# Transposes and eight column tiles of a later projection beside the first token mixing, dense rounds of eight chunks, other gather rates

## The chip, the cores and the metric

The kernel runs on one core of a Trainium2 chip. The metric is the device time of one execution in microseconds (us), the median of several runs. The engines are TensorE (PE in the rows, with its weight loads as PEld), VectorE (DVE), ScalarE (ACT), GpSimd (POOL) and SyncE (SP), and 16 DMA engines move data between HBM and the on-chip memories SBUF and PSUM. "Clock" is the TensorE clock that the chip granted, as a share of full speed.

## The reference, cut

One decoder layer over 1024 tokens of width 1024, in float32:

```python
x = layer_norm(x)                                    # ln_in
proj = x @ w_in                                      # 3592 columns: fq fk fv ff hq hf hi hg
fox = causal_softmax(fq fk^T / 8 + c_t - c_s) @ fv   # 8 heads of 64, c = cumsum(log_sigmoid(ff))
hgrn = gated recurrence(hq, hf, hi)                  # 4 heads, 128x128 state, chunkwise
mix = concat(rms(fox), rms(hgrn) * silu(hg)) @ w_out
x = layer_norm(alpha * x + mix)                      # ln_mix
q = (x @ w_q)                                        # 8 heads x 2 halves x 128
s = q . sub_keys                                     # 128 scores per half
idx, best = top16(top16(s half 0) + top16(s half 1)) # of 128*128 experts, per head
gates = softmax(best)                                # 8 heads x 16 = 128 experts a token
h = gelu(x . u_tab[idx]) * gates
y = sum over the 128 experts of h * v_tab[idx]
return layer_norm(alpha * x + y)                     # ln_ffn
```

## The kernel before

**Precision.** A large product is three float32r matmuls: an operand is split into a hi part (a copy by ACT, float32r) and a lo part (raw minus hi, by DVE or POOL), and `mm3` (L281) issues hi*hi, hi*lo and lo*hi. `weight` (L204) loads a 128x1024 slice of weights into `wraw` on SP's queue, lets ACT make `whi`, and lets DVE or, by a counter and `WDIV`, POOL make `wlo`.

**Groups of tokens.** `mixers` (L311) goes through three groups: tokens 0 to 255, 256 to 767 and 768 to 1023. The first group's x is layer-normed, transposed and projected alone (T = 256); then comes its chain, `fox` and `hgrn`, the output projection with its layer norm `mix_out`, and the selection of experts, `select` and `select_tail`. Only then are the 768 later tokens projected, all at once: `project` (L407) transposes x from four tiles that `preload` had loaded (six tiles of 128 tokens, each eight 128x128 transposes by PE, hi by ACT and lo by DVE or POOL), and `project_cols` (L434) makes 17 column tiles m (24 matmuls of 512 columns and 24 of 256 each, by `projT`, evacuated by ACT at L451) and six groups of `wn` (`projN`, evacuated at L482). Then follow the second and the third group's chains, mixes and selections.

**Experts in two ways.** Tokens of blocks 0, 1, 6 and 7 (`GATHER`) fetch their experts' rows one by one: `gather_rows` (L1090) is an indirect DMA that POOL issues, 128 rows of 1024 (0.524 MB), into one of eight buffers `rows`. In `gather_u` (L1109) DVE multiplies such a row by x and sums it into `sd`; in `gather_v` DVE adds h times the row to `ys` in SBUF (L1134) for the blocks of `VDVE`, 1, 6 and 7, and for block 0 PE does the sum in PSUM. That is 512 u rows, 384 v rows on DVE and 128 on PE. Tokens of blocks 2 to 5 (`DENSE`) go through all 16384 experts in 128 chunks of 128: `up` (L1020) loads a chunk of u, splits it (uh by ACT, ul by DVE), makes the scores, gelu, multiplies by the gates `gt`, which `gbuild` had written to HBM, and splits into hh and hl; `down` (L1037) loads the chunk's v in two halves of 512 columns, splits (vh, vl), and sums into PSUM over a round of `JG` = 4 chunks; at a round's end DVE adds the four accumulators to `dy` (L1049). A round's `down` runs beside the next round's `up`.

**What sets the order.** The gathers are jobs that `tick` (L175) pulls forward: each stage of the program calls `tick` at its steps, and the table `RATE` says how many u rows, v rows and steps of `gbuild` a call pulls. In the dense part a tick is a chunk, 5.4 rows each; ticks of the first round, which stands over the last selection's tail, count `W0` = 0.71. `HOLD` holds the u rows back for some ticks after the first tail. From the program a scheduler makes one fixed order for each engine, and each engine runs its own in that order.

**PSUM.** One tile `y` of 128x1024 in the pool `psy` (single buffer) serves the sums on PE of block 0; `psf`, `psh` and `psv` are the other banks.

## Time and profile before

| | us |
|---|---|
| three runs | 3128.02, 3137.72, 3138.84 |
| median | 3137.72 |
| the profiled execution, whole | 3098.22 |
| its span on the core | 3096.5 |

The mean granted clock in the profiled execution is 0.918. From the start of the span the stages are, in us:

| stage | from | to |
|---|---|---|
| layer norm and projection of the first group | 0 | 123 |
| its chain, mix and layer norm | 123 | 239 |
| its selection and tail | 239 | 358 |
| transposes of the later x | 303 | 335 |
| projection of 768 tokens | 337 | 589 |
| second group | 589 | 1042 |
| third group: chain | 1042 | 1263 |
| mix, selection, gate build | 1263 | 1521 |
| dense part | 1521 | 3076 |
| last layer norm and store | 3076 | 3096.5 |

In the rows, a busy time in a stretch is the time in which an engine had at least one instruction; "x" is a count; "<-" names what released a wait. A timeline row has start, duration, engine, line, operation, output <- inputs and shapes.

### The profile page before, as it was taken

What the parts mean: (1) busy time and instruction counts of PE and PEld (TensorE: products, weight loads), DVE (VectorE), ACT (ScalarE), POOL (GpSimd) and SP (SyncE); (2) the same over time, 40 slices, a digit from 0 to 9 for tenths busy, and PEclk for the clock granted to TensorE, in tenths of its full rate; (3) what the DMA queues carried; (4) which work ended last, traced back from release to release, by engine and by line L of the source; (5) the groups of instructions that cost most, each with busy time, mean ns of one, the idle gap of its engine ahead of it and who ended that gap; (6) DMA issues with size and microseconds to landing.
All of it is one profiled execution on the core that took longest, in us unless ns stands there. A gap on an engine that the chain in (4) does not pass through costs nothing.

```text
span 3096.5 us, 45624 instructions
## 1 busy us (share of the span) xinstructions
PE 2614.4 (84%) x16057; PEld 2150.2 (69%) x16057; DVE 2707.3 (87%) x5573; ACT 1097.2 (35%) x2028; POOL 1678.8 (54%) x1240
## 2 busy tenths in 40 slices
PE   6778799777779768777569999899989999999995
...
DMA  7632599754978858763489999999999999999994
GB/s 269 198 137 89 184 336 330 241 162 151 350 253 290 290 164 298 256 249 144 186 280 342 346 377 360 340 366 361 350 344 367 381 379 357 357 370 342 370 336 159
DMA packets 338662, 887.13 MB, mean 286 GB/s; under 512 B 29912, under 2 KB 124136, under 8 KB 336000
## 3 DMA queue, kind: packets, MB, share of 16 engines
...
q8 instruction: 126, 2.06, 0.3%
...
## 4 chain that ended last, share of the span: by engine, by line
DVE 40%; PE 36%; issue 11%; DMA 6%; ACT 4%; POOL 3%; SPq 0%; DVEq 0%; POOLq 0%; ACTq 0%
DVE ys L1134 8%; DVE rows L1109 6%; PE psf L284 6%; PE psf L285 5%; PE psf L283 5%; PE psh L285 4%; PE psh L283 4%; PE psh L284 4%; DMA rows<-in_v,gsel 2%; POOL rows L1090 2%; DVE dy L1049 2%; DVE vl L1017 1%; DVE ohj L947 1%; DVE tw L793 1%; DVE al L947 1%
## 5 line engine op out<-in xcount | busy, mean ns | idle before, releaser
L1090 POOL DMA_INDIRECT rows<-in_u,gsel x512 | 689.7, 1347 | 481.8 <-DVE rows L1109 302.5
L1090 POOL DMA_INDIRECT rows<-in_v,gsel x512 | 637.9, 1246 | 433.3 <-DVE ys L1134 264.5
L1109 DVE SCALAR_TENSOR_TENSOR rows<-rows,gx 128x1024 f32<-128x1024 f32 x512 | 629.8, 1278 | 38.6 <-DMA rows<-in_u,gsel 25.3
L1134 DVE SCALAR_TENSOR_TENSOR ys<-rows,sd,ys 128x1024 f32<-128x1024 f32 x381 | 491.2, 1289 | 0.6
L283 PE MATMUL psh<-dxh,uh 128*128 128x512 f32 x1024 | 402.8, 393 | 28.9 <-ACT uh L1016 16.1
L285 PE MATMUL psh<-dxh,ul 128*128 128x512 f32 x1024 | 400.8, 391 | 9.5 <-DVE ul L1017 9.4
L284 PE MATMUL psh<-dxl,uh 128*128 128x512 f32 x1024 | 400.3, 391 | 0.0
L284 PE MATMUL psf<-vl,hh 128*128 128x512 f32 x768 | 312.3, 407 | 42.9 <-DVE vl L1017 42.1
L1016 ACT ACTIVATE vh<-vr 128x512 fp32r<-128x512 f32 x256 | 161.8, 632 | 435.8 <-PE psv L285 408.7
L285 PE MATMUL psf<-vh,hl 128*128 128x512 f32 x768 | 307.7, 401 | 0.0
L283 PE MATMUL psf<-vh,hh 128*128 128x512 f32 x768 | 279.1, 395 | 11.9 <-DVE dy L1049 9.7
L1016 ACT ACTIVATE uh<-ur 128x1024 fp32r<-128x1024 f32 x128 | 136.0, 1062 | 410.6 <-PE psh L284 408.9
L213 POOL TENSOR_TENSOR wlo<-wraw,whi 128x1024 fp32r<-128x1024 f32 x70 | 181.8, 2603 | 154.1 <-ACT whi L210 145.7
L283 PEld LDWEIGHTS psh<-dxh,uh 128*128 128x128 f32 x1024 | 193.5, 189 | 76.8 <-ACT hs L1030 20.3
L285 PEld LDWEIGHTS psh<-dxh,ul 128*128 128x128 f32 x1024 | 193.4, 189 | 50.6 <-DVE ul L1017 10.5
L210 ACT ACTIVATE whi<-wraw 128x1024 fp32r<-128x1024 f32 x130 | 136.9, 1056 | 250.8 <-PE psf L284 64.1
L284 PEld LDWEIGHTS psh<-dxl,uh 128*128 128x128 f32 x1024 | 193.6, 189 | 39.7
L284 PEld LDWEIGHTS psf<-vl,hh 128*128 128x128 f32 x768 | 148.7, 194 | 90.2 <-DVE vl L1017 59.4
L1017 DVE TENSOR_TENSOR vl<-vr,vh 128x512 fp32r<-128x512 f32 x256 | 170.6, 688 | 14.0 <-ACT vh L1016 13.9
L283 PEld LDWEIGHTS psf<-vh,hh 128*128 128x128 f32 x768 | 145.5, 190 | 50.1 <-DVE dy L1049 10.0
L213 DVE TENSOR_TENSOR wlo<-wraw,whi 128x1024 fp32r<-128x1024 f32 x60 | 81.8, 1365 | 111.0 <-ACT whi L210 111.0
L285 PEld LDWEIGHTS psf<-vh,hl 128*128 128x128 f32 x768 | 149.1, 194 | 30.2
(337 smaller groups left out, 6354.4 us busy)
## 6 DMA issues: line engine op xcount, KB each, us to landing
ur<-in_ut SPq DMA_DIRECT2D x128, 512.0 KB
vr<-in_v SPq DMA_DIRECT2D x256, 256.0 KB
...
```

The source lines that it names most:

```text
L210: nc.scalar.activation(hi, raw, AF.Copy)
L213: eng.tensor_tensor(lo, raw, hi.bitcast(F32), op=ALU.subtract)
L283: mm(out, lh, rh, start=start, stop=False, **kw)
L284: mm(out, lh, rl, start=False, stop=False, **kw)
L285: mm(out, ll, rh, start=False, stop=stop, **kw)
L947: eng.tensor_tensor(t.rearrange("p t (m c) -> p t m c", c=2), x, y, op=op)
L1016: nc.scalar.activation(hi, raw, AF.Copy)
L1017: nc.vector.tensor_tensor(lo, raw, hi.bitcast(F32), op=ALU.subtract)
L1049: nc.vector.tensor_tensor(y[:, tb, ns], y[:, tb, ns], acc[tb], op=ALU.add)
L1090: self.nc.gpsimd.indirect_dma_start(out=t, out_offset=None, in_=tab, in_offset=bass.IndirectOffsetOnAxis(ap=idx, axis=0))
L1109: self.pin(nc.vector.scalar_tensor_tensor(u, u, 1.0, x2, op0=ALU.mult, op1=ALU.mult, accum_out=sd[:, n : n + 1]), "u")
L1134: self.pin(nc.vector.scalar_tensor_tensor(ys, v, h, ys, op0=ALU.mult, op1=ALU.add), "w")
```

## The change

**A generator `early`** makes the transposes and the column tiles m = 0 to 7 (`NEARLY`) of the 768 later tokens. Each x tile and each raw, hi and lo weight is now a `rows` buffer, which no gather uses at that time, and the transposes and the tile's sums both go to `y` in PSUM; all its lo parts are DVE's. It is pulled by `tick` during the first group's chain, mix and selection, at the rates `ERATE`, and drained before the first tail. `project_cols` then makes tiles 8 to 16 for the later tokens. `preload` and the transposes in `project` are gone.

**The dense part** goes in rounds of `JG` = 8 chunks, so `dy` is added to once in eight chunks; gates come in pieces of four chunks (`GT`); the hh and hl buffers are 12 slots (`HSL`) in two pools; raw v buffers are 4 and not 5 (`VRAW`). The gain and bias of the last layer norm are loaded into row buffers by each `finish` and into `ur` buffers by the last, where they stood in buffers of their own.

**The sum over v rows** of blocks 1, 6 and 7 has its accumulator `ys` in PSUM (the tile `y`) and not in SBUF.

**The rates** of gathers and gate build change in most stages, and `HOLD` is 4 for 7.

```diff
@@ -29,23 +29,25 @@
 RATE = {
-    "proj": {768: (4.0, 5.39, 0), 256: (0, 0, 0)},
-    "fox": {512: (1.0, 1.0, 0), 256: (0, 3.99, 3.59)},
+    "proj": {768: (5.6, 0, 0), 256: (0, 0, 0)},
+    "fox": {512: (1.0, 0.4, 0), 256: (1.2, 4.5, 3.59)},
     "hgrn": {512: (0, 0, 0), 256: (0, 0, 0)},
-    "mix": {512: (3, 1, 0), 256: (0, 1, 6)},
-    "sel": {512: (2, 2, 0), 256: (0, 0.72, 3.75)},
-    "dense": (5.4, 5.4, 0),
+    "mix": {512: (3, 1, 0), 256: (0, 0, 6)},
+    "sel": {512: (2, 2, 0), 256: (0, 0, 3.75)},
+    "dense": (5.0, 5.0, 0),
 }
 VDVE = (1, 6, 7)
-HOLD = 7
+HOLD = 4
...
+NEARLY = 8
+ERATE = {"fox": 0.55, "hgrn": 0.0, "mix": 0.25, "sel": 0.19}
...
-JG = 4
+JG = 8
+GT = 4
+HSL = 12
...
+        self.ahead, self.due = None, 0.0
...
@@ -173,6 +177,12 @@
         yield
 
     def tick(self, phase, T=None, w=1.0):
+        if self.ahead and phase in ERATE:
+            self.due += w * ERATE[phase]
+            while self.due >= 1.0:
+                self.due -= 1.0
+                next(self.ahead, None)
+            return
         rate = RATE[phase] if T is None else RATE[phase][T]
         self.hold = max(self.hold - w, 0.0)
         for n, q in enumerate((self.ujobs, self.vjobs, self.bjobs)):
@@ -309,7 +319,7 @@
         return po
 
     def mixers(self, groups, es):
-        st, gb, tl = ExitStack(), ExitStack(), ExitStack()
+        st, gb, tl, ex = ExitStack(), ExitStack(), ExitStack(), ExitStack()
         self.lx = ExitStack()
         init = self.setup()
         next(init)
@@ -323,6 +333,11 @@
             st.close()
             if n < 2:
                 tl.close()
+            ex.close()
+            if n == 0:
+                pa = ex.enter_context(self.pool("pa", 1, "right"))
+                x1 = [pa.tile([P, DC, S - T], F32R, name=m, tag=m) for m in ("xh", "xl")]
+                self.ahead = self.early(T, S - T, *x1, pa)
             po = st.enter_context(self.pool("po", 1, "left"))
             mh = po.tile([P, DC, T], F32R, name="mh", tag="mh")
             ml = po.tile([P, DC, T], F32R, name="ml", tag="ml")
@@ -347,8 +362,6 @@
             si = pz.tile([P, nq, 16, 16], U32, name="si", tag="si")
             best = pz.tile([P, nq, 8, 16], F32, name="best", tag="best")
             pos = pz.tile([P, nq, 8, 16], U32, name="pos", tag="pos")
-            if n == 0:
-                x1 = self.preload(T, S - T)
             self.select(t0, T, mh, ml, sv, si, best, pos, T == 256 or EARLY)
             if late:
                 self.drain(self.bjobs)
@@ -360,8 +373,8 @@
                 dense = self.dense_prep(es)
             pw = tl.enter_context(self.pool("pw", 1, "right"))
             if n == 0:
-                x1 = self.project(T, S - T, st, x1)
-                self.lx.close()
+                self.drain([self.ahead])
+                self.ahead = None
             tail = self.select_tail(t0, T, sv, si, best, pos, T == 256 or EARLY, pw)
             if T == 256:
                 tail = self.tail_gather(t0, T, tail)
@@ -412,31 +425,49 @@
         def split(n, x):
             self.transpose_split("f", x, xh, xl, n)
 
-        if t0:
-            with self.pool("pt", 2, "right") as pt:
-                for n, x in enumerate(xs):
-                    self.transpose_split("f", x, xh, xl, n, pt if n % 2 < PSPL else None)
-        else:
-            pl = self.lx.enter_context(self.pool("pl", 2, "left"))
-            self.first_ln(pl, 0, T, split)
-            self.lns = [lambda r0=r0: self.first_ln(pl, r0, 2 * P, lambda n, x: None) for r0 in range(T, S, 2 * P)]
+        pl = self.lx.enter_context(self.pool("pl", 2, "left"))
+        self.first_ln(pl, 0, T, split)
+        self.lns = [lambda r0=r0: self.first_ln(pl, r0, 2 * P, lambda n, x: None) for r0 in range(T, S, 2 * P)]
         return xh, xl
 
-    def preload(self, t0, T):
-        pl = self.lx.enter_context(self.pool("pl", 1, "left"))
-        xs = []
+    def early(self, t0, T, xh, xl, pa):
+        nc, a = self.nc, self.a
         for n in range(T // P):
-            x = pl.tile([P, D], F32, name="x", tag="x", bufs=T // P)
+            x = self.rows()
             self.q("x1l").dma_start(x, self.d_x1[t0 + n * P : t0 + (n + 1) * P])
-            xs.append(x)
-        return xs
+            pt = self.psy.tile([P, D], F32, name="y", tag="y")
+            for c in range(DC):
+                nc.tensor.transpose(pt[:, c * P : (c + 1) * P], x[:, c * P : (c + 1) * P], self.ident)
+            sl = slice(n * P, (n + 1) * P)
+            for c0 in range(0, DC, 4):
+                v = pt[:, c0 * P : (c0 + 4) * P].rearrange("p (c t) -> p c t", c=4)
+                h = xh[:, c0 : c0 + 4, sl]
+                nc.scalar.activation(h, v, AF.Copy)
+                nc.vector.tensor_tensor(xl[:, c0 : c0 + 4, sl], v, h.bitcast(F32), op=ALU.subtract)
+            yield
+        for m in range(NEARLY):
+            raw, hi, lo = self.rows(), self.rows(F32R), self.rows(F32R)
+            self.q("w").dma_start(raw, a["wt"][m])
+            nc.scalar.activation(hi, raw, AF.Copy)
+            nc.vector.tensor_tensor(lo, raw, hi.bitcast(F32), op=ALU.subtract)
+            wh, wl = (t.rearrange("p (c m) -> p c m", c=DC) for t in (hi, lo))
+            po = self.psy.tile([P, D], F32, name="y", tag="y")
+            s = pa.tile([P, T], F32, name="es", tag="es", bufs=2)
+            for c0 in range(0, T, 512):
+                cs = slice(c0, min(c0 + 512, T))
+                for dc in range(DC):
+                    self.mm3(po[:, cs], wh[:, dc], wl[:, dc], xh[:, dc, cs], xl[:, dc, cs], dc == 0, dc == DC - 1)
+                nc.scalar.activation(s[:, cs], po[:, cs], AF.Copy, scale=0.125 if m < 4 else 1.0)
+            h = m % 4
+            self.q("qk").dma_start((self.d_q, self.d_k)[m // 4][h * P : (h + 1) * P, t0 : t0 + T], s)
+            yield
 
     def project_cols(self, t0, T, xh, xl):
         nc, a = self.nc, self.a
         nq = T // P
         tsl = slice(t0, t0 + T)
         with self.pool("pb", 2, "right") as pb:
-            for m in range(17):
+            for m in range(NEARLY if t0 else 0, 17):
                 po = self.projT(self.weight(pb, a["wt"][m], "p1" if t0 else "p0"), xh, xl, T)
                 self.tick("proj", T)
                 if m in LNM and self.lns:
...
+            def hslot(m):
+                pool, k, bufs = (dw, "", JG) if m % HSL < JG else (dv[0], "2", HSL - JG)
+                return [pool.tile([P, TD], F32R, name=n + k, tag=n + k, bufs=bufs) for n in ("hh", "hl")]
+
             def up(g):
-                gt = dw.tile([P, TD // 32, JG, 32], F32, name="gt", tag="gt")
-                nc.sync.dma_start(gt, self.d_g[:, :, g * JG : (g + 1) * JG, :].rearrange("q j i t -> j q i t"))
                 for c in range(JG):
-                    hh, hl = (dw.tile([P, TD], F32R, name=n, tag=n, bufs=JG + 2) for n in ("hh", "hl"))
+                    if c % GT == 0:
+                        gt = dw.tile([P, TD // 32, GT, 32], F32, name="gt", tag="gt")
+                        i0 = g * JG + c
+                        nc.sync.dma_start(gt, self.d_g[:, :, i0 : i0 + GT, :].rearrange("q j i t -> j q i t"))
+                    hh, hl = hslot(g * JG + c)
                     uh, ul = (t.rearrange("p (c j) -> p c j", c=DC) for t in split(dw, a["ut"][g * JG + c], D, "u", 2, 3))
                     ps = self.bank("h")[:, :TD]
                     for dc in range(DC):
@@ -1029,7 +1066,7 @@
                     hs = dw.tile([P, TD], F32, name="hs", tag="hs")
                     nc.scalar.activation(hs, ps, AF.Gelu)
                     h3 = hs.rearrange("p (q t) -> p q t", t=32)
-                    nc.vector.tensor_tensor(h3, h3, gt[:, :, c], op=ALU.mult)
+                    nc.vector.tensor_tensor(h3, h3, gt[:, :, c % GT], op=ALU.mult)
                     nc.scalar.activation(hh, hs, AF.Copy)
                     nc.vector.tensor_tensor(hl, hs, hh.bitcast(F32), op=ALU.subtract)
                     yield hh, hl
@@ -1054,7 +1091,6 @@
                 yield from tail
                 tl.close()
                 dv[0] = dws.enter_context(self.pool("dv", 2, "left"))
-                self.lnf = self.ffn_rows([dv[0].tile([P, D], F32, name=n, tag=n, bufs=1) for n in ("dlg", "dlb")])
 
             late, c0 = late(), 0
             prev = iter(())
@@ -1078,12 +1114,13 @@
                 self.drain([late])
                 if g == NG - 1:
                     dv[1] = dv[0].tile([P, ND, 2, 6], F32, name="lnst", tag="lnst", bufs=1)
+                    gb = self.ffn_rows([dw.tile([P, D], F32, name="ur", tag="ur", bufs=3) for _ in range(2)])
                 if h:
                     prev = down(g, h)
-            self.finish_dense(dv[0], y, dv[1])
-
-    def rows(self):
-        return self.gp.tile([P, D], F32, name="rows", tag="rows", bufs=NROWS)
+            self.finish_dense(dv[0], y, dv[1], gb)
+
+    def rows(self, dt=F32):
+        return self.gp.tile([P, D], dt, name="rows", tag="rows", bufs=NROWS)
 
     def gather_rows(self, tab, idx):
         t = self.rows()
@@ -1119,7 +1156,7 @@
         nc.scalar.activation(sd, sd, AF.Gelu)
         nc.vector.tensor_tensor(sd, sd, gt, op=ALU.mult)
         if blk in VDVE:
-            ys = gp.tile([P, D], F32, name="ys", tag="ys")
+            ys = self.psy.tile([P, D], F32, name="y", tag="y")
             ei = sel[:, 0].bitcast(I32)
             vs = []
             for k in range(P + LAG):
...
```

The order of instructions on PE within the first group's chain, of before (L667 to L701 are `fox`'s scores and transposes, L595 is `hgrn`, `k`, `q`, `pr`, `v` and `pt` their operands):

```order
L595 MATMUL psh<-v,scT_198 128x128
L704 MATMUL psv<-v,pt 128x128
L727 MATMUL psf<-ident,o 128x128 x2
L667 MATMUL psf<-k,q_1554 128x256
L670 LDWEIGHTS identb
L670 MATMUL psf<-cmaskb,identb 128x128
L701 MATMUL psf<-ident,pr 128x128
L667 MATMUL psf<-k,q_1553 128x128
```

And on PE at such a place of after, where L698 to L735 are `fox` and L651 is `hgrn`, and L293 to L295 are `mm3`, here with a column tile's hi and lo weights in `rows` and its sum in `y`:

```order
L294 MATMUL y<-xl,rows 128x512
L295 MATMUL y<-xh,rows 128x512
L732 MATMUL psf<-ident,pr 128x128
L698 MATMUL psf<-k,q_1558 128x256
L701 LDWEIGHTS identb
L701 MATMUL psf<-cmaskb,identb 128x128
L651 MATMUL psh<-ident,ov 128x128
L293 MATMUL y<-xh,rows 128x256
```

A column tile's matmuls of 512 and of 256 columns stand between the small matmuls of the chain. All 48 transposes and 308 of the 384 matmuls of the eight tiles stand ahead of the first matmul of `select`, the other 76 within it.

DVE's order in the tail of the first selection, of before (L857 to L915 are the tail's steps, L213 is the lo part of a weight for the later projection):

```order
L873 SCALAR_TENSOR_TENSOR ptm<-pf,ptm 128x128
L882 TENSOR_TENSOR oh<-oh 128x256
L874 TENSOR_TENSOR ab<-plo,ptm 128x8x16
L883 TENSOR_TENSOR ij<-oh 128x128
L213 TENSOR_TENSOR wlo<-wraw,whi 128x1024
L897 SCALAR_TENSOR_TENSOR eo<-ij 128x128
L857 CAST fi<-si 128x256
L878 TENSOR_TENSOR oh<-ab,i_3644 128x2048
L912 CAST sel<-eo 128x128
```

And of after at the tail's end (L913 to L946 are the tail, L223 the weights' lo, L1146 the first u rows):

```order
L914 TENSOR_TENSOR ij<-oh 128x128
L946 COPY sel<-gt 128x128
L928 SCALAR_TENSOR_TENSOR eo<-ij 128x128
L223 TENSOR_TENSOR wlo<-wraw,whi 128x1024
L943 CAST sel<-eo 128x128
L945 CAST sel<-psh 128x128
L223 TENSOR_TENSOR wlo<-wraw,whi 128x1024
L1146 SCALAR_TENSOR_TENSOR rows,sd<-rows,gx_4437 128x1024 x3
```

The first lo part of a weight that DVE makes for the later projection stands 23 rows ahead of the first u row in before and 4 rows ahead of it in after, behind nearly all of the tail. Tile 8's lo part is POOL's.

DVE's order in the dense part, of before, where the round of four chunks ends (L1134 a v row, L1032 and L1034 the `hs` and `hl` of an up chunk, L1049 the additions to `dy`):

```order
L1032 TENSOR_TENSOR hs<-hs,gt 128x512
L1134 SCALAR_TENSOR_TENSOR ys<-rows,sd,ys 128x1024
L1034 TENSOR_TENSOR hl<-hs,hh 128x512
L1134 SCALAR_TENSOR_TENSOR ys<-rows,sd,ys 128x1024
L1049 TENSOR_TENSOR dy<-dy,psf 128x512
L1134 SCALAR_TENSOR_TENSOR ys<-rows,sd,ys 128x1024
L1049 TENSOR_TENSOR dy<-dy,psf 128x512
L1134 SCALAR_TENSOR_TENSOR ys<-rows,sd,ys 128x1024
```

And of after at the like depth of the dense part (L1171 a v row, L1048 the lo parts of u and v, L1069 and L1071 the up chunk):

```order
L1171 SCALAR_TENSOR_TENSOR y<-rows,sd,y 128x1024 x4
L1069 TENSOR_TENSOR hs<-hs,gt 128x512
L1048 TENSOR_TENSOR ul<-ur,uh 128x1024
L1071 TENSOR_TENSOR hl<-hs,hh 128x512
L1171 SCALAR_TENSOR_TENSOR y<-rows,sd,y 128x1024
L1048 TENSOR_TENSOR vl<-vr,vh 128x512
L1171 SCALAR_TENSOR_TENSOR y<-rows,sd,y 128x1024
L1048 TENSOR_TENSOR vl<-vr,vh 128x512
L1171 SCALAR_TENSOR_TENSOR y<-rows,sd,y 128x1024 x3
```

The additions to `dy` (256 in before, 128 in after) are half as many, and more v rows stand directly behind one another (17 such rows in before, 87 in after, counted over the whole order). Of u rows, 282 stand in the dense part of DVE's order and not 312; 25 and not 4 in the third group's chain.

## Rows read from the trace of the kernel before

**Rows 1.** The page: busy us of engines; DMA share in 40 slices.

```profile
PE 2614.4 (84%) x16057; PEld 2150.2 (69%) x16057; DVE 2707.3 (87%) x5573; ACT 1097.2 (35%) x2028; POOL 1678.8 (54%) x1240
...
DMA  7632599754978858763489999999999999999994
```

**Rows 2.** Busy us by stage: stretch, length; PE PEld DVE ACT POOL; clock, DMA share, GB/s.

```profile
123.00:239.00 116.00, 76.58 (x837) 66.99 (x837) 68.68 (x181) 50.13 (x120) 48.01 (x38) 0.72 0.43 151
239.00:303.00 64.00, 58.08 (x450) 57.51 (x449) 55.29 (x317) 22.85 (x43) 31.17 (x13) 0.92 0.26 83
303.00:337.00 34.00, 9.72 (x48) 7.29 (x46) 33.41 (x141) 11.67 (x23) 8.72 (x7) 0.64 0.11 38
337.00:589.00 252.00, 248.62 (x1682) 230.44 (x1682) 157.57 (x245) 61.57 (x84) 171.15 (x115) 0.99 0.87 310
1042.00:1263.00 221.00, 154.09 (x1652) 100.14 (x1652) 193.61 (x759) 98.62 (x269) 102.39 (x108) 0.86 0.76 252
1521.00:1600.00 79.00, 39.44 (x148) 30.55 (x149) 56.67 (x114) 18.26 (x24) 21.26 (x15) 0.74 0.72 238
1600.00:3000.00 1400.00, 1341.12 (x5750) 1084.83 (x5749) 1354.84 (x1827) 410.35 (x604) 883.36 (x654) 0.98 0.98 359
```

**Rows 3.** Costliest groups of DVE, 1600 to 3000: busy us, mean ns | idle before.

```profile
L1134 DVE SCALAR_TENSOR_TENSOR ys<-rows,sd,ys 128x1024 f32<-128x1024 f32 x353 | 455.4, 1290 | 0.6
L1109 DVE SCALAR_TENSOR_TENSOR rows<-rows,gx 128x1024 f32<-128x1024 f32 x297 | 346.5, 1222 | 11.7 <-DMA gx<-d_x 8.5 <-DMA rows<-in_u,gsel 3.2
L1017 DVE TENSOR_TENSOR vl<-vr,vh 128x512 fp32r<-128x512 f32 x242 | 161.0, 688 | 8.4 <-ACT vh L1016 8.4
...
L1049 DVE TENSOR_TENSOR dy<-dy,psf 128x512 f32<-128x512 f32 x180 | 118.2, 681 | 0.2 <-PE psf L285 0.2
```

**Rows 4.** Waits, 1600 to 3000: us in total, times, longest us.

```profile
POOL rows L1090 <- DVE ys L1134: 245.9, 260, 6.8
...
PE psf L284 <- DVE vl L1017: 40.3, 23, 8.5
```

**Rows 5.** Timeline of PE at 2404 us, eight matmul starts apart: start, duration.

```profile
2404.27 0.39 PE L285 MATMUL psf<-vh,hl 128*128 128x512 f32 x1
...
2406.09 0.39 PE L284 MATMUL psv<-vl,hh 128*128 128x512 f32 x1
```

**Rows 6.** Columns of rows 2, two stretches with the highest rate of transfers.

```profile
2500.00:2600.00 100.00, 95.98 (x418) 77.64 (x417) 99.01 (x119) 29.34 (x44) 60.28 (x49) 1.00 1.01 380
360.00:380.00 20.00, 20.00 (x126) 18.10 (x125) 7.03 (x10) 6.41 (x10) 13.37 (x12) 1.00 1.02 395
```

**Rows 7.** Timeline of DVE in the dense part: start, duration; rows in sequence.

```profile
2100.70 1.28 DVE L1134 SCALAR_TENSOR_TENSOR ys<-rows,sd,ys 128x1024 f32<-128x1024 f32 x1
2101.89 0.68 DVE L1049 TENSOR_TENSOR dy<-dy,psf 128x512 f32<-128x512 f32 x1
2102.49 1.28 DVE L1134 SCALAR_TENSOR_TENSOR ys<-rows,sd,ys 128x1024 f32<-128x1024 f32 x1
...
2138.62 2.60 DVE L1134 SCALAR_TENSOR_TENSOR ys<-rows,sd,ys 128x1024 f32<-128x1024 f32 x2
...
2405.42 1.22 DVE L1109 SCALAR_TENSOR_TENSOR rows<-rows,gx 128x1024 f32<-128x1024 f32 x1
2406.56 1.22 DVE L1109 SCALAR_TENSOR_TENSOR rows<-rows,gx 128x1024 f32<-128x1024 f32 x1
```

**Rows 8.** ACT's evacuations in the projection: ns min/median/max, first and last start.

```profile
L451 ACT ACTIVATE s<-psf x5: 599/599/601, 407.5 to 440.9; 128x512 f32<-128x512 f32 x5
...
L482 ACT ACTIVATE s<-psh x6: 597/598/598, 502.8 to 590.1; 128x512 f32<-128x512 f32 x6
```

**Rows 9.** Timelines: transposes, PE's start of the projection, the tail's last cast.

```profile
325.70 3.67 PE L270 MATMUL psf<-ident,x 128*128 128x128 f32 x16 [3.44 <-DVE xl L279]
...
336.88 0.80 PE L283 MATMUL psf<-xh,whi 128*128 128x512 f32 x1 [4.73 <-ACT whi L210]
...
357.80 0.29 DVE L914 CAST sel<-psh 128x128 int32<-128x128 f32 x1
```

9 lines of the change are left out of this document (4 added, 5 removed).

## The prediction

> **What bounds the kernel now.** I read the page first, then the busy time of every engine by stage, and then the stage that is half of the span. On the page PE and DVE are busy 84% and 87% of the span, and the DMA line stands at 9 from the middle to the end [rows 1]. The stages tell these averages apart [rows 2]. From 123 to 239 us (the first group's chain, its output projection and layer norm) no engine is full: PE 77 of 116 us, DVE 69, DMA share 0.43, granted clock 0.72, a mixture of the two levels. From 239 to 337 us (the first selection and its tail) DVE is full from the first scores on, while PE has 10 of the last 34 us. From 337 to 589 us (the later tokens' projection) PE has 249 of 252 us and the transfers a share of 0.87. From 1600 to 3000 us, the dense part, three things are full at once: PE 1341 and DVE 1355 of 1400 us, DMA share 0.98 at 359 GB/s.
>
> For the dense part I work per chunk of 128 experts. In these 1400 us DVE makes 242 vl, two a chunk: 121 chunks, **11.57 us a chunk**, with 353 + 297 = 650 gathered rows, 5.4 a chunk [rows 3]. PE's longest waits are for DVE's vl (40 us), and POOL's are for DVE to free a row buffer (246 us) [rows 4]: DVE is late, its next is never. What each would need alone: PE starts a 512-column matmul every 1.82 / 8 = 0.2275 us [rows 5], 48 a chunk, 10.9 us. DVE: 1355 busy us over 121 chunks, 11.2 us. DMA: 5.4 gathers of 0.524 MB, 0.524 MB of u, 0.524 of v and 0.262 of gates, 4.14 MB; at 359 GB/s 11.5 us, at the 380 of the best stretch 10.9 [rows 6]. Every engine is near full, and the real pace is 3% over DVE's own 11.2.
>
> **Dense rounds of eight chunks.** dy is added once in 8 chunks and not in 4: one 128x512 add a chunk instead of two. Each occupies DVE 0.60 us, start to next start [rows 7]. The rate falls from 5.4 to 5.0 gathers a tick; a tick is a chunk, so 0.4 of a gather less: 0.4 x 1.19 us on DVE (a V row at 2100.70, its next at 2101.89) and 0.21 MB. That works because 30 u rows move ahead: DVE's order has 282 of 512 of them in the dense part and not 312, with 384 V in both; (282 + 384) / 5.0 = 133.2 ticks, and there are 16 rounds of 8 and 8 ticks ahead of them that count 0.71 each, 133.7. DVE then needs 11.2 - 0.60 - 0.48 = 10.1 us, DMA 3.93 MB or 10.3 us at 380 GB/s, PE still 10.9. PE is next. With the same 3% over the largest I take 11.2 us a chunk: 0.37 x 121 = -45 us. Bounds: 10.9, PE without a wait, -81 us; 11.45, three near-full engines still colliding, -15.
>
> The first round has 8 up chunks over the select tail where it had 4. DVE does 57 of these 79 us and PE 39 [rows 2]; the round needs DVE for the tail, 28 u rows of 1.14 us [rows 7] and 8 chunks' splits, some 80 us in all by my estimate, and PE has then done half of 8 chunks where it has now done 3.1 in 79 us: about -4. The gates' rows for ln_ffn are loaded by each of three finishes again, 3.1 MB, 9 us of transfer at 359 GB/s, free while DMA isn't last. Fewer vr buffers (4 for 5) I cost at nothing: PE's waits there name DVE and not a load [rows 4]; if that cover goes it is in the upper bound. Dense: **-49** (-85 to -15).
>
> **V sums in PSUM.** ys moves from SBUF to y, for 384 rows, as source and as destination. No DVE instruction of before writes PSUM. The nearest row is dy, with one source in PSUM: 681 ns against 688 for vl of the same size with none [rows 3]. I take no difference. What changes by order alone: 87 V now stand right behind a V, which were 17, and a pair takes 2.60 us, so the second ends 0.13 us later than after another instruction [rows 7]: +9 us on DVE, 0.07 a chunk, below PE's 10.9. Bounds from -0.01 to +0.13 us for each V; even the upper end leaves DVE at 10.8. [...]
>
> **Transposes and 8 tiles beside the first chain.** Removed: from 303 to 337 us the transposes, and eight of 17 column tiles. A tile's evacuations are (440.9 - 407.5) / 4 = 8.35 us apart, a wn group's 17.5 [rows 8]; the eight are 67 us. Added beside the chain: PE 67 + some 12 for 48 transposes (0.25 us each, as 16 take 3.67 in the stretch of the old ones), ACT and DVE a hi and a lo per tile, 6 loads of x rows and 8 of weights on SP at a DMA share of 0.43. By PE's order 6.4 of the 8 tiles and all transposes stand ahead of the first select tile, so 65 us of PE fall into the 116, where 39 are idle [rows 2]. Were the idle time filled to the last, the stretch grows by 26; were the granted clock then full, the 77 us of its own shrink by some 12, so 15 at best; were nothing hidden, 65. I take **35**, nearer the low end, because most of the tiles stand in single waits of the chain and in the layer norm's gap. New waits: ACT's hi waits for its weight with the chain's exponentials queued behind it, and PE waits for ACT to empty y, of which there is one; both are in the 35. The other 1.6 tiles stand in the selection, where DVE is last: nothing.
>
> What then starts the projection is DVE's tail. Before, PE began at 336.88 and the tail's last selection index was cast at 357.80 [rows 9]. Now the first DVE split (wlo) stands behind nearly the whole tail, and tile m = 8 alone has its split on POOL. The tail ends at 358 - 6 (no xl, one split less) + 35 = 387. PE then needs 8 tiles and 6 groups, 8 x 8.35 + 6 x 17.4 = 171 us. But 109 gathers that the order has here (57 MB), 18 weights (9) and the outputs (8) are 74 MB, at 375 GB/s, a little under the 380 and 395 that are seen [rows 6], 197 us: the transfers bind. End at 584 and not 589: **-5** (-28 to +25).
>
> **Key gathers.** 25 u rows stand in the third chain on DVE, which had 4: 21 x 1.14 = 24 us, where DVE has 221 - 194 = 27 idle [rows 2] in small waits. I take half, **+12** (0 to +24). Fewer V in the second chain cost nothing: they are PE's and POOL's, neither is full there.
>
> **Sum.** -49 - 5 + 12 = -42 us against the profiled execution's 3098.2. The three runs have a median 1.3% higher, 3137.7, so -42 counts as -43: **3095 us**.
>
> **Rivals.** (1) *The transfers stay last.* For: share 0.98 now and a projection with 74 MB in 170 us of PE. Against: 380 GB/s over 100 us [rows 6]. At 359 GB/s a chunk takes 10.95 x 1.03 = 11.28, the projection ends 9 us later, the reloads cost 9: -35 - 4 + 4 + 12 + 9 = -14, 3124. [...] (2) *The chain hides nothing* (+65) and all 21 rows are paid: -49 + 25 + 24 = 0, 3138. (3) *PE's floor is reached* and the chain grows by 15: -85 - 25 + 0 = -110, 3026. (4) **Slower**: *the PSUM sum has a long turn-around.* Each V reads what the last wrote; from SBUF that costs 0.13 us [rows 7]. DVE becomes last again once a V takes 1.34 us (4.2 + 5 x 1.34 = 10.9), and the kernel is slower by over 0.5% from about 1.46 us on; at 1.55 the chunk is 11.95 x 1.03 = 12.3, +88 + 7, 3234. Against it: 681 ns for dy. That the tiles are not moved at all is excluded by PE's order.
>
> **Chances.** Forecast 0.45, its own range 3070 to 3118; (1) 0.18; (2) 0.13; (3) 0.14; (4) 0.10. A measurement tells 0.5%, 16 us, from no change. Faster: nearly all of the forecast (0.44), (3) and under half of (1) (0.08), 0.66; same: the rest of the forecast and of (1) and most of (2), 0.22; slower: (4) and the worst of (2), 0.12. Range 3032 to 3142: it leaves out half of (3), (4) and the worst of (2), 0.19.
>
> **What would show it.** In the dense stretch: 11.2 us a chunk, DVE under 95% busy, PE's waits for vl gone, V at 1.19 to 1.25 us from start to start. In the projection: PE idle between tiles and DMA share near 1. From 123 to 239: mix and layer norm ended 35 us later. In the third chain DVE over 92% busy. Wrong if V is over 1.3 us, if the chain grows by over 60, or if PE still waits for vl.

## The result

The changed kernel takes 3149.15 us (median of 8 runs, 3138.39 to 3165.81), the kernel before 3132.12 (8 runs, 3126.91 to 3138.84): a ratio on record of 1.0064, with a 95% interval of 1.0045 to 1.0083 (the two medians alone give 1.0054). It is slower by 17 us by the medians, where 43 us less were forecast and a loss had a chance of 0.12. The profiled execution took 3138.39 us, its span is 3136.6.

In some sets of runs (kernels that ran together on one chip) the kernel before takes 3088 to 3093 us, called a short set below, and in others 3129 to 3132, a long set; it isn't the chip alone, since the first two sets of experiments, one short and one long, ran on the same one. By two traces of the kernel before, nearly the whole difference lies in the third group's chain (206 us of 3098 in the one, 246 of 3135 in the other). The trace behind [rows 1 to 9] has the short form (3098 us), while the timed runs beside it, by their times, have the long one.

The page of the changed kernel, against [rows 1]:

```profile
PE 2624.0 (84%) x16057; PEld 2156.3 (69%) x16057; DVE 2655.8 (85%) x5454; ACT 1090.1 (35%) x2021; POOL 1601.5 (51%) x1231
...
DMA  8544299865868887664359999999999999999996
```

DVE has 51 us less to do, as was meant. The dip of the DMA line ahead of the dense part reads 4, 3, 5 in slices 19 to 21, where [rows 1] has 3, 4, 8: at 78 us a slice, something ahead of the dense part grew. The busy time by stage, columns as in [rows 2]:

```profile
123.00:239.00 116.00, 96.45 (x978) 83.86 (x979) 63.30 (x169) 60.46 (x141) 38.98 (x33) 0.90 0.35 119
...
337.00:589.00 252.00, 195.92 (x1366) 183.00 (x1365) 197.40 (x418) 53.72 (x80) 172.86 (x118) 0.89 0.80 298
1042.00:1263.00 221.00, 167.92 (x1505) 99.05 (x1506) 168.37 (x592) 75.63 (x200) 124.33 (x121) 0.80 0.78 259
1521.00:1600.00 79.00, 31.40 (x324) 28.18 (x324) 62.57 (x166) 31.57 (x59) 0.00 (x0) 0.69 0.44 175
1600.00:3000.00 1400.00, 1333.29 (x5745) 1090.78 (x5746) 1266.43 (x1683) 414.22 (x611) 772.95 (x611) 0.97 0.96 347
```

The first chain's stretch took in the early tiles at a better clock (0.90 for 0.72). The projection has PE 196 us busy and not 249. From 1521 to 1600 us, where the dense part stood before, POOL now does nothing at all: the kernel is still building gates.

The fair pair is the kernel before and the changed one profiled beside each other (experiments e9 and e10, a long set). Ends of the stages in us, each the end of the last instruction of its line:

| end of | before (e9) | changed (e10) | later by |
|---|---|---|---|
| first mix | 224 | 256 | 32 |
| first selection | 302 | 346 | 44 |
| projection of 768 | 589 | 587 | -2 |
| second selection | 1040 | 1033 | -7 |
| third chain's sums | 1286 | 1280 | -6 |
| third selection | 1490 | 1499 | 9 |
| gate build | 1560 | 1597 | 37 |
| dense part's last dy | 3113 | 3124 | 11 |
| span | 3133 | 3146 | 13 |

So 7 us were gained up to the second selection's end and 26 in the dense part, and 43 us were lost between the third chain's end and the gate build's.

### The profile page after: what moved, and what is told of

It is laid out like the page before. It is cut to its first block, busy times and chain, and to the rows that moved or that the text cites. A ratio compares the mean times of both kernels' runs of the same rounds, so it can differ in the third digit from the quotient of the medians.

```text
span 3136.6 us, 45362 instructions
## 1 busy us (share of the span) xinstructions
PE 2624.0 (84%) x16057; PEld 2156.3 (69%) x16057; DVE 2655.8 (85%) x5454; ACT 1090.1 (35%) x2021; POOL 1601.5 (51%) x1231
## 4 chain that ended last, share of the span: by engine, by line
PE 33%; issue 6%; DVE 6%; DMA 2%; POOL 2%; ACT 1%; POOLq 0%; SPq 0%; DVEq 0%; ACTq 0%
PE psh L295 5%; PE psh L294 5%; PE psh L293 5%; PE psf L294 4%; PE psf L295 4%; PE psf L293 4%; POOL rows L1127 2%; PE psv L295 1%; PE psv L294 1%; DVE rows L1146 1%; PE psv L293 1%; DVE y L1171 1%; DMA rows<-in_u,gsel 1%; DMA rows<-in_v,gsel 1%; DMA vr<-in_v 0%
## 5 line engine op out<-in xcount | busy, mean ns | idle before, releaser
L1127 POOL DMA_INDIRECT rows<-in_u,gsel x512 | 676.9, 1322 | 514.3 <-DVE rows L1146 339.8
L1127 POOL DMA_INDIRECT rows<-in_v,gsel x512 | 587.8, 1148 | 495.2 <-DVE y L1171 359.2
L1146 DVE SCALAR_TENSOR_TENSOR rows<-rows,gx 128x1024 f32<-128x1024 f32 x512 | 641.8, 1292 | 87.0 <-DMA rows<-in_u,gsel 77.3
L1171 DVE SCALAR_TENSOR_TENSOR y<-rows,sd,y 128x1024 f32<-128x1024 f32 x381 | 489.0, 1283 | 3.7 <-DMA rows<-in_v,gsel 0.5
L293 PE MATMUL psh<-dxh,uh 128*128 128x512 f32 x1024 | 401.6, 392 | 21.7 <-ACT uh L1047 16.1
L295 PE MATMUL psh<-dxh,ul 128*128 128x512 f32 x1024 | 400.8, 391 | 8.7 <-DVE ul L1048 8.6
L295 PE MATMUL psf<-vh,hl 128*128 128x512 f32 x768 | 305.2, 397 | 0.0
L293 PE MATMUL psf<-vh,hh 128*128 128x512 f32 x768 | 296.9, 397 | 10.0 <-DVE dy L1086 8.9
L223 POOL TENSOR_TENSOR wlo<-wraw,whi 128x1024 fp32r<-128x1024 f32 x67 | 169.6, 2540 | 252.5 <-ACT whi L220 239.6
L293 PEld LDWEIGHTS psh<-dxh,uh 128*128 128x128 f32 x1024 | 193.6, 189 | 62.7 <-ACT uh L1047 16.3
L295 PEld LDWEIGHTS psh<-dxh,ul 128*128 128x128 f32 x1024 | 193.7, 189 | 50.0 <-DVE ul L1048 9.7
L220 ACT ACTIVATE whi<-wraw 128x1024 fp32r<-128x1024 f32 x122 | 127.7, 1055 | 208.5 <-PE psf L294 53.1
L1048 DVE TENSOR_TENSOR ul<-ur,uh 128x1024 fp32r<-128x1024 f32 x128 | 156.4, 1222 | 51.5 <-ACT uh L1047 47.9
L1048 DVE TENSOR_TENSOR vl<-vr,vh 128x512 fp32r<-128x512 f32 x256 | 170.5, 685 | 25.8 <-ACT vh L1047 25.6
L293 PEld LDWEIGHTS psf<-vh,hh 128*128 128x128 f32 x768 | 146.3, 191 | 47.6 <-DVE dy L1086 11.9
L295 PEld LDWEIGHTS psf<-vh,hl 128*128 128x128 f32 x768 | 148.1, 193 | 30.8
```

The lines of the kernel that those rows point to most:

```text
L220: nc.scalar.activation(hi, raw, AF.Copy)
L223: eng.tensor_tensor(lo, raw, hi.bitcast(F32), op=ALU.subtract)
L293: mm(out, lh, rh, start=start, stop=False, **kw)
L295: mm(out, ll, rh, start=False, stop=stop, **kw)
L1048: nc.vector.tensor_tensor(lo, raw, hi.bitcast(F32), op=ALU.subtract)
L1127: self.nc.gpsimd.indirect_dma_start(out=t, out_offset=None, in_=tab, in_offset=bass.IndirectOffsetOnAxis(ap=idx, axis=0))
```

## The experiments

**Theory A** says that the planner's account is lost. `tick` adds to `owed` on every call, up to 16, whether there are jobs or not:

```python
self.owed[n] = min(self.owed[n] + w * rate[n], 16.0)
while self.owed[n] >= 0.5 and q:
```

In the kernel before, the first group's own chain has a gate rate of 3.59 and no gate jobs yet, so it fills the account to 16 steps, which the third chain spends at its start on the second tail. In the changed kernel `tick` returns early there, and the account is 0. In the trace of before, DVE starts 10 of its 232 one-hot steps (L947) ahead of the third chain's end and 54 ahead of the last row of the third mix; in the trace of after (L978) it starts none ahead of either. One kind of them in the two traces (ns min/median/max, first to last start):

```profile
L947 DVE TENSOR_TENSOR ohi<-iota16h,gpair x64: 660/682/2881, 1239.7 to 1510.8; 128x1024 f16<-128x1024 f16 x64
```

```profile
L978 DVE TENSOR_TENSOR ohi<-iota16h,gpair x64: 661/682/2872, 1334.1 to 1577.3; 128x1024 f16<-128x1024 f16 x64
```

**Theory B** says that the u rows in the third chain, with their gathers, are the loss. The first set is a short one (the kernel before: 3088.07 us).

**e1: the account alone.**

```diff
                 self.ahead = None
+                self.owed[2] = 16.0
```

> The changed kernel with one line more: after the first group, 16 steps of gate work are put to the planner's account, which the kernel before had collected in its first group and the changed kernel does not (its tick returns early there). Theory A (the lost account starts the second tail and the gate build later, and all that is left of the build stands alone ahead of the dense part): the build starts inside the third chain, 25 of its 240 one-hot steps move ahead of the third mix, and the dense part starts some 30 us earlier, 3149 - 30 = 3119. Theory B (the u rows and their gathers in the third chain are the loss): the account only reorders the tail, the chain stays some 40 us longer than before, 3149 to 3140.

3124.16 us, 1.0101 [1.0074, 1.0128] of before. The 54 one-hot steps stand ahead of the third mix's end again, and from the chain's end (1284 us) to the build's it takes 286 us, for 315 in the trace of after. But the chain has 256 us, as long as theory B has it. The build's matmuls, first to last start (the shape in the middle is one half's):

```profile
L1004 PE MATMUL psh<-ah,ohj x512: 216/219/330, 1278.9 to 1569.5; 128*128 128x128 f16 x171
```

**e2: the kernel before without the account.**

```diff
         for n, (t0, T) in enumerate(groups):
+            self.owed[2] = 0.0
```

> The kernel before with that account set to zero at each group. Theory A: the gate build starts after the third mix as in the changed kernel, the lone stretch of it grows from 72 to some 104 us, 3132 + 31 = 3163. Theory B: no change, 3132, since no u row is moved.

3123.82 us, 1.0099 [1.007, 1.0128]: +31 us as ratio, from a line that takes no gather across a stage (688 of 1024 in the dense part, as before). The time between the third chain's end and the gate build's end is 311 us, where it is 274 in both traces of before; the chain itself is some 12 us shorter (194 us for 206), with less of the tail's work in it. Of the one-hot steps 26 still start ahead of the third mix's end, so theory A's place for them was missed: the account is worth 28 of the 54.

**e3: the old rates of the third group.**

```diff
-    "fox": {512: (1.0, 0.4, 0), 256: (1.2, 4.5, 3.59)},
+    "fox": {512: (1.0, 0.4, 0), 256: (0, 3.99, 3.59)},
-    "mix": {512: (3, 1, 0), 256: (0, 0, 6)},
-    "sel": {512: (2, 2, 0), 256: (0, 0, 3.75)},
-    "dense": (5.0, 5.0, 0),
+    "mix": {512: (3, 1, 0), 256: (0, 1, 6)},
+    "sel": {512: (2, 2, 0), 256: (0, 0.72, 3.75)},
+    "dense": (5.2, 5.2, 0),
```

> The changed kernel with the rates of before for the third group's chain, mix and selection (u 0, v 3.99, then v 1 and 0.72), so that the 21 u rows go back to the dense part, whose rate is 5.2 for 5.0 to take them in; the account stays at zero. Theory B: the third chain falls from 243 to some 204 us, 3149 - 39 = 3110. Theory A: the chain's length is mostly its own tail's and the gain is under 15, 3135 or more.

3103.4 us, 1.0047 [1.0025, 1.0069]. The third chain has 196 us, and from its end to the build's it takes 314 us, as in the changed kernel. Its stretch, columns as in [rows 2]:

```profile
1025.00:1221.00 196.00, 147.47 (x1535) 92.88 (x1527) 164.39 (x676) 80.58 (x215) 102.08 (x106) 0.87 0.81 268
```

**e4: both,** the edits of e1 and e3 together.

> Both at once: account of 16, old rates in the third group, dense rate 5.2. Theory A and B add up if they are separate losses: 3149 - 31 - 39 = 3079, and the third group then takes as long as before (486 us from its first chain instruction to the dense part). If they are one and the same loss, 3110 to 3119 as with one of them.

3080.04 us, 0.9957 [0.9937, 0.9977]: faster than the kernel before. The execution that was traced took 3095.66 us. The gate build's matmuls in e3 and in e4:

```profile
L1003 PE MATMUL psh<-ah,ohj x512: 216/230/330, 1262.7 to 1534.5; 128*128 128x128 f16 x171
```

```profile
L1004 PE MATMUL psh<-ah,ohj x512: 216/219/330, 1248.1 to 1529.2; 128*128 128x128 f16 x171
```

From the second selection's end (1025 and 1041 us) to the build's end e3 takes 510 us and e4 489: the account is worth 21 there, as e2 has 505 against 480 in the trace of before. That e1 stays above the kernel before with the same account while e4 falls below it shows that the rates matter too. The third chain's stretch in e4 and in e1, columns as in [rows 2]:

```profile
1041.00:1251.00 210.00, 146.03 (x1561) 94.70 (x1554) 182.24 (x731) 85.00 (x231) 103.99 (x107) 0.85 0.75 244
```

```profile
1028.00:1284.00 256.00, 175.00 (x1640) 104.20 (x1639) 211.67 (x776) 87.17 (x232) 138.90 (x134) 0.79 0.76 260
```

In the same stretch of e1, the wait that costs PE most (us in total, times, longest us):

```profile
PE y L1200 <- DMA rows<-in_v,gsel: 41.0, 16, 6.7
```

With the new rates the stretch has 46 us more, and PE stands 41 us for gathered v rows (6.5 us in the trace of before). The second set is a long one (before: 3128.8 us).

**e5: the changed kernel again.**

> The changed kernel itself beside the experiments below, so that they have a common neighbour: 1.0064 of the kernel before, by the result. Theory A (lost account) and theory B (u rows in the third chain) expect the same here.

3146.38 us, 1.0056 [1.0035, 1.0077].

**e6: the u rows apart from the v rows.** The edit of e1, and:

```diff
-    "fox": {512: (1.0, 0.4, 0), 256: (1.2, 4.5, 3.59)},
+    "fox": {512: (1.0, 0.4, 0), 256: (0, 4.5, 3.59)},
-    "dense": (5.0, 5.0, 0),
+    "dense": (5.2, 5.2, 0),
```

> The changed kernel with the account of 16 and with one rate changed, the u rows in the third chain (0 for 1.2); the v rows keep the new 4.5, then 0 and 0. Dense rate 5.2. If the u rows are what lengthens the third chain and takes the account's gain: as with all old rates, 0.996 of the kernel before, the chain near 205 us, the dense part starting 55 to 60 us earlier than in the changed kernel. If the denser v rows (4.5 for 3.99) do it: the chain stays near 240 us and the time near 1.006.

3136.67 us, 1.0022 [1.0006, 1.0037]. The chain is 255 us with no u row in it but the 4 that the kernel before has as well. So the u rows alone aren't the cost; but this is a long set, and a chain of the kernel before was still to be seen in one (e9: 246 us).

**e7: rounds of four.**

```diff
-JG = 8
+JG = 4
-HSL = 12
+HSL = 6
```

> The changed kernel with rounds of four chunks in the dense part again (JG 4, 6 slots for hh and hl), all else as changed. By the prediction's step (one 0.60 us add a chunk more on DVE, which then has 10.7 us a chunk and stands under PE's 10.9): little of the pace comes back, +0 to +0.1 us a chunk, 0 to 13 us, since the 0.4 row a chunk less is kept. If the adds of dy to PSUM banks are what PE waits for at a round's end: +0.25 us a chunk, +32 us.

3179.91 us, 1.015 [1.0123, 1.0176]: 34 us slower than e5 beside it by the medians, 29 by the ratios. The pace (the start of the 16th vl to that of the 240th, over 112 chunks) is 11.457 us a chunk for 11.266: 0.19, more than I expected, where four traces of the changed kernel itself lie between 11.266 and 11.335. And at this rate the v rows don't end with the chunks: the last one starts 18 us behind the last dy, where in e5 it is 5 us ahead of it.

**e8: the PSUM sum alone, in the kernel before.**

```diff
-            ys = gp.tile([P, D], F32, name="ys", tag="ys")
+            ys = self.psy.tile([P, D], F32, name="y", tag="y")
```

> The kernel before with the sum of the v rows in PSUM and not in SBUF, nothing else. The prediction's value: no difference for a V, 3132 by the result or 1.000. [...] A long turn-around (V at 1.46 us and over): 1.03 or more.

3166.64 us, 1.0117 [1.0094, 1.014]. The pace is 11.838 us for the 11.603 of e9, also a long set. The V rows themselves are no slower. In the timeline of DVE in e8 (start, duration):

```profile
2115.03 1.28 DVE L1134 SCALAR_TENSOR_TENSOR y<-rows,sd,y 128x1024 f32<-128x1024 f32 x1
2116.22 0.68 DVE L1049 TENSOR_TENSOR dy<-dy,psf 128x512 f32<-128x512 f32 x1
2116.82 1.28 DVE L1134 SCALAR_TENSOR_TENSOR y<-rows,sd,y 128x1024 f32<-128x1024 f32 x1
```

1.19 us from a V to the next start, and 0.60 for a dy, both as in [rows 7]. So the loss of pace (some 28 us over 121 chunks) isn't in the V rows. What changed is the order that the scheduler made: 169 of DVE's 5573 instructions stand at another place. DVE's waits from 1720 to 3020 us in e8, and the same group in e9:

```profile
DVE ul L1017 <- ACT uh L1016: 18.8, 10, 4.4
```

```profile
DVE ul L1017 <- ACT uh L1016: 2.3, 2, 2.1
```

Waits for ACT are some 25 us longer in all (45 for 20, over `ul`, `vl`, `hl` and `hs`), and DVE is busy 1234 of the 1300 us there (PE 1228). That the other order causes them is argued and not shown.

**The third set** (long, before 3128.76) puts the kernel before beside the changed one. Its theory C speaks of the chip; by the sets the form changes from set to set.

**e9: the kernel before.**

> The kernel before, profiled on the same chip as the next three. Its third chain took 204 us in the trace that the prediction was read from (3098 us), while the timed runs beside the result are 34 us longer. Theory C (the third chain of one and the same program takes about 200 or about 245 us by the chip it runs on): where the kernel before is near 3130 its chain is near 245 here, and then the chain of the changed kernel is no longer than that. Theory B (the new rates make it long): its chain is near 204 beside a changed kernel with 243 or more.

3134.88 us. The chain, from the second selection's end to the last sum:

```profile
1040.00:1286.00 246.00, 168.01 (x1566) 106.15 (x1565) 183.44 (x735) 86.96 (x232) 103.03 (x108) 0.78 0.64 210
```

And PE's wait for gathered v rows in it:

```profile
PE y L1162 <- DMA rows<-in_v,gsel: 6.9, 3, 4.6
```

**e10: the changed kernel beside it.**

> The changed kernel beside it. Theory B: third chain 243 to 250 us on any chip, 35 to 45 longer than that of the kernel before, 1.006. Theory C: both chains long (or both near 200); what is left against the kernel before is the gate build, +31 us, against the dense part's -27.

3147.03 us, 1.0073 [1.0037, 1.011]. The same two views of its third chain:

```profile
1033.00:1280.00 247.00, 176.81 (x1595) 104.05 (x1593) 193.28 (x713) 81.64 (x215) 139.06 (x133) 0.81 0.78 266
```

```profile
PE y L1199 <- DMA rows<-in_v,gsel: 27.6, 12, 6.2
```

246 against 247 us: in a long set the chain of the changed kernel is no longer, though the new rates put 103 gathers into it and not 78. That doesn't show that the rates cost nothing: the chain of e10 has lost the account's work as well, which is worth 12 us of chain in e2, so a cost of the rates can hide behind it. The program of e9 is that of [rows 1 to 9] and took 206 us there (from the second selection's end at 1039 us):

```profile
1039.00:1246.00 207.00, 144.77 (x1574) 94.97 (x1574) 182.65 (x731) 86.22 (x235) 102.13 (x106) 0.87 0.75 246
```

The gate build's matmuls, e9 and e10:

```profile
L972 PE MATMUL psh<-ah,ohj x512: 216/219/330, 1282.0 to 1559.7; 128*128 128x128 f16 x171
```

```profile
L1003 PE MATMUL psh<-ah,ohj x512: 216/229/330, 1346.1 to 1596.6; 128*128 128x128 f16 x171
```

It starts 64 us later and ends 37 us later.

**e11: account and old rates, again.**

> Account of 16 and the old rates of the third group in the changed kernel, again: 0.996 of the kernel before on either kind of chip, if what it gains is the account (28 to 31 us) and the third chain as in the kernel before. Theory B: its chain is 35 to 45 us shorter than the changed kernel's beside it; theory C: no shorter where the chip is slow.

3121.19 us, 0.9976 [0.9961, 0.9992]. The chain is 244 us, near both neighbours, and from its end to the build's end it takes 280 us and not the 317 of e10. The dense part, from the first ul to the last dy, is 1527 us for 1510, with 21 u rows more in it and a rate of 5.2. From e6, also in a long set, this kernel differs by the v rates alone (3.99 for 4.5, then 1 and 0.72 for 0), and e6 has 1.0022 with a chain 11 us longer:

```profile
1029.00:1284.00 255.00, 177.85 (x1647) 116.28 (x1647) 183.53 (x732) 87.17 (x232) 115.38 (x115) 0.78 0.68 220
```

```profile
1032.00:1276.00 244.00, 168.56 (x1573) 106.91 (x1572) 184.20 (x735) 87.61 (x235) 103.12 (x108) 0.78 0.65 214
```

So the denser v rows cost a long chain something, beside the same account.

**e12: no early tiles.** As e11, with:

```diff
-NEARLY = 8
+NEARLY = 0
```

> The same with no column tiles beside the first chain (the transposes stay there). The prediction: the first mix ends some 25 us earlier, the projection has 8 more tiles of 8.35 us, 67 us of PE, but only as far as transfers don't bind it (197 us): about 35 to 45 us later at the projection's end, 1.01 of the kernel before. If the early tiles gain nothing: the same time as its neighbour.

3178.82 us, 1.016 [1.0123, 1.0196]. The projection's last evacuations in e11 and in e12:

```profile
L514 ACT ACTIVATE s<-psh x6: 597/598/602, 487.6 to 590.3; 128x512 f32<-128x512 f32 x6
```

```profile
L514 ACT ACTIVATE s<-psh x6: 597/598/602, 531.9 to 646.4; 128x512 f32<-128x512 f32 x6
```

The first mix ends at 230 us and not 254, and the projection 56 us later. That is more than I expected: at a rate of 5.6 u rows a tick, the eight ticks more bring their own gathers (333 GB/s from 337 to 589 us, for 294 in e11), so the 56 us hold both.

**The fourth set** (short, before 3089.02) asks what holds the dense part, and looks for more. **e13: gates loaded in the first round only.**

```diff
-                    if c % GT == 0:
+                    if c % GT == 0 and g == 0:
...
+                        gts.append(gt)
+                    gt = gts[c // GT]
```

> The changed kernel, in which only the first round of the dense part loads gates and the later rounds use the first round's again: each chunk has 0.262 MB less to transfer, and every instruction of PE, DVE, ACT and POOL stays. Theory D (the transfers hold the dense part): the pace falls from 11.31 to the next limit, 10.9 to 11.05 us a chunk, 30 to 45 us over 120 chunks. Theory E (PE with its waits holds it, as the prediction put it): 11.25 to 11.3, under 8 us.

3124.2 us, 1.0114 [1.0088, 1.0139]. The pace is 11.307 us, as in e10. The dense stretch of e10 and of e13:

```profile
1720.00:3020.00 1300.00, 1263.28 (x5479) 1035.85 (x5478) 1191.17 (x1553) 389.60 (x575) 729.26 (x585) 0.98 0.97 354
```

```profile
1720.00:3020.00 1300.00, 1266.71 (x5510) 1039.69 (x5509) 1196.77 (x1551) 391.81 (x578) 737.25 (x586) 0.98 0.93 333
```

With 6% less moved (333 for 354 GB/s), and with DVE's and ACT's order unchanged, the pace stays: the transfers don't hold the part. What is left is PE, 97% busy in both; that PE holds it is argued from this share, since no run takes work off PE alone. Rival (1) had its time a chunk nearly right (11.28) for a reason that is wrong.

**e14: two products of three in down.**

```diff
-                            self.mm3(acc[tb], hs[c][0][:, ts], hs[c][1][:, ts], vh, vl, c == 0, c == JG - 1)
+                            nc.tensor.matmul(acc[tb], hs[c][0][:, ts], vh, start=c == 0, stop=False)
+                            nc.tensor.matmul(acc[tb], hs[c][0][:, ts] if tb < 2 else hs[c][1][:, ts], vl if tb < 2 else vh, start=False, stop=c == JG - 1)
```

> The changed kernel with two of the three products in the dense part's down sums (hi*lo kept for two token blocks, lo*hi for the other two, so every tile is still made and read): 40 matmuls of 512 columns a chunk and not 48, PE 9.1 us and not 10.9; no transfer and no DVE instruction less. Theory D: the pace stays near 11.2. Theory E: it falls to the next limit, DVE's 10.4 or the transfers' 11.0, and by 0.3 us or more.

3189.98 us, 1.0327 [1.0299, 1.0355]: slower, with less to do.

```profile
1720.00:3020.00 1300.00, 1096.04 (x4356) 851.92 (x4355) 1124.69 (x1489) 368.06 (x549) 735.27 (x559) 0.91 0.94 338
```

PE's waits in that stretch:

```profile
PE psv L1083 <- DVE dy L1087: 74.5, 15, 19.4
PE psf L1084 <- DVE vl L1048: 65.4, 25, 5.9
```

The pace is 11.823 us. PE now waits for `dy` and `vl`, and its clock is 0.91. The edit changed the scheduler's order as well (322 of DVE's 5454 instructions stand elsewhere), so this run doesn't decide between the theories.

**e15: an account of 32.** As e4, with:

```diff
-            self.owed[n] = min(self.owed[n] + w * rate[n], 16.0)
+            self.owed[n] = min(self.owed[n] + w * rate[n], 32.0)
...
-                self.owed[2] = 16.0
+                self.owed[2] = 32.0
```

> Account of 32 steps for 16, with the old rates of the third group and dense rate 5.2 as in the run with both. If the lone gate build is a plain loss that idle DVE time in the third chain and mix can take (183 of 246 us busy): 43 one-hot steps fewer stand in it, some 15 to 28 us earlier, 0.990 of the kernel before. If the third mix is already full (PE waits for the one-hots and DVE for its layer norm): what is gained in the build is lost in the mix, 0.997 as with 16.

3098.78 us, 1.003 [1.0016, 1.0045]. From the third selection's end to the build's end it falls from 71 to 44 us, but the third chain takes 238 us for the 211 of e4. What is gained in the build is lost, as in the second case, though in the chain and not in the mix, and more than all of it.

**e16: u rows in the third mix.** As e4, with:

```diff
-    "mix": {512: (3, 1, 0), 256: (0, 1, 6)},
+    "mix": {512: (3, 1, 0), 256: (2, 1, 6)},
-    "dense": (5.2, 5.2, 0),
+    "dense": (5.0, 5.0, 0),
```

> Account of 16 and old rates, but with 23 u rows in the third mix and selection's start (rate 2 in the mix), where PE takes few v rows, and the dense rate 5.0 again. If the u rows only cost where PE takes v rows beside them: dense 1512 and not 1529 us, the mix 5 to 15 us longer, 0.994 to 0.998. If they cost wherever DVE is near full: 24 us of DVE more ahead of the gate build, 1.000 or more.

3107.49 us, 1.0059 [1.0036, 1.0082]: the second case. The chain has 206 us, but the build ends at 1544 us, 514 behind the second selection's end and not 489, and the dense part takes 1518 us and not 1512.

**The last set** (short, before 3092.52). **e17: the changed kernel in a short set.**

> The changed kernel. Where the kernel before is near 3088: third chain 238 to 245 us against its 194 to 204, and 1.011 to 1.014 of it. Where the kernel before is near 3130: 1.0065 as before, chain 247 against 246.

3137.49 us, 1.0165 [1.0127, 1.0203]. The third chain's stretch and the wait for v rows:

```profile
1031.00:1263.00 232.00, 167.95 (x1600) 98.19 (x1599) 194.03 (x718) 82.03 (x215) 135.90 (x133) 0.84 0.83 284
```

```profile
PE y L1199 <- DMA rows<-in_v,gsel: 29.9, 15, 6.0
```

The chain is 232 us, 6 less than I expected, and some 26 more than the 206 of before from the same end. With the account at zero on both sides, the old rates have 196 us (e3) and the new ones 232, and with the account 211 (e4) and 256 (e1): in short sets the rates cost the chain 36 to 45 us, and the lost account hides some 12 of it where the changed kernel stands beside the one before. So theory B holds in a short set. In a long one the fair pair can't show it, and the share of the v rows is 11 us (e6 against e11).

**e18: u rows in the second chain.** As e4, with:

```diff
-    "fox": {512: (1.0, 0.4, 0), 256: (0, 3.99, 3.59)},
+    "fox": {512: (1.4, 0.4, 0), 256: (0, 3.99, 3.59)},
-    "dense": (5.2, 5.2, 0),
+    "dense": (5.0, 5.0, 0),
```

> Account of 16, old rates in the third group, and some 20 u rows more in the second chain (rate 1.4 for 1.0), so that the dense rate is 5.0 again. If DVE's free 38 us there take them: dense 1512 and not 1529 us, second chain 211 as it was, 0.990 of the kernel before where e4 has 0.996, 0.993 where it has 0.998. If the u rows lengthen a chain wherever they stand: second chain 10 to 20 us longer, no better than without.

3096.66 us, 1.0023 [1.0003, 1.0043]. The dense part is 1514 us, as wanted, but the second chain takes 233 us for the 216 of e4. What the rate saves in the dense part, the chain pays.

## Why the prediction was wrong

**Dense rounds of eight: half the size.** -49 was forecast; the part (start of the first ul to that of the last dy) fell from 1536.5 to 1509.7 us in the fair pair, -27, and the end behind it takes 2 more. The pace was the better part: 11.57 to 11.20 forecast, 11.603 to 11.309 measured, -36 over 121 chunks against -45. By the prediction's own 3%, 10.92 us of PE give 11.25 and not 11.2, so some 5 of these 9 us are a rounding. The rest is the "same 3%" of waits, which is 3.6%: PE's own wait for DVE's `vl` alone is 20 us of the 1300 in e10, not gone as "What would show it" has it, and PE is idle 37 us there. The larger error lies in the first round and the ends: -4 was forecast and +9 came. The last v row now starts 5.5 us behind the last vl, where it was 14 us ahead of it, and the last dy starts 10.9 us behind the last vl and not 5.4. That DVE has room now is right (1191 of 1300 us busy, 92%); that PE is next is argued from e13.

**V sums in PSUM: right for the row,** 1.19 us and 2.60 for a pair in e8 (four in a row take 5.25 in e10), so rival (4) falls. Its threshold was also worked out too low: it charges all five rows of a chunk, where by the prediction's own counts 384 of 666, 2.9 a chunk, are V. In the kernel before the same edit costs 1.2% all the same (e8), in an order that differs; that the order is the cause isn't shown, and no run has the changed kernel with this sum in SBUF, so what the edit costs there stays open. A part of the 22 us that the dense part lacks may come from it.

**Transposes and eight tiles: right, and the rows fit the mechanism.** The two levels of the granted clock that the prediction mixes to 0.72 stand in the trace of before: 0.50 from 147 to 175 us and 1.00 from 207 to 227. The first mix ended 32 us later (35 forecast), the first tail's last cast started at 385 us (387), the projection ended at 587 (584, -2 and not -5). From 384 to 587 us PE is busy 179 of 203 us in e10 and the DMA share is 0.95, which fits transfers that bind, at 354 GB/s and not 375; no run takes gathers alone out of this stage. In e12, where the tiles stand in the projection and their ticks bring more gathers, it ends 56 us later.

**Key gathers: the step that failed.** I took +12 (0 to +24), by the 21 u rows on DVE alone; from the second selection's end to the gate build's the fair pair lost 44 us. Two things were left out that the runs show. First, the account: the diff shows the early return in `tick`, and the kernel's text says that rates are pulled by calls; I counted rows and never the gate build's steps. It is worth 25 us from the second selection's end to the build's in e2 (31 by ratio) and 21 from e3 to e4. It acts behind the chain: from the chain's end to the build's it takes 286 us with the account alone put back (e1), 314 with the old rates alone (e3) and 315 to 318 in the changed kernel; the chain itself is 12 to 24 us shorter without it (e2, e3 for e4, e17 for e1). Second, what the new rates do to the chain: 36 to 45 us in short sets, by e3 against e17 and e4 against e1, one trace each. The new rates with the account weren't run in a long set, so what they cost there is known for the v rows alone (11 us, e6 against e11).

Why the rates cost that much is in part argued. PE's v rows stand in the chain's own order, and a row that lands late holds the chain: PE waits for them 28 to 30 us in e10 and e17 (16 to 18 in the traces of the result and of e5), for 7 in before and 12 in e3. But e6 has a chain of 255 us with only 8 us of these waits, so they aren't the whole. DVE's idle 27 us were taken as room, and "What would show it" wanted DVE over 92% busy in the third chain; it is busy 193 of 247 us there, 78%. None of the rivals had any of this: the slower one was the wrong mechanism.

**The rule of 1.3% between trace and median** hid the form of the third chain: 206 us in the trace, and 246 in a trace of a long set (e9), where the timed runs by their times belong.

The sum in the fair pair: -7 to the second selection, +1 in the chain, +43 from there to the build's end (of which the account is the larger part, by e1's 286 us for 315 to 318), -26, +2, +13 us in all.

**A version that beats both** is the changed kernel with the account put back and the old rates in the third group (e4, e11): 0.9957 and 0.9976 of the kernel before, both intervals under 1.
